# Holding TensorE to the order of the source in a two-layer encoder, while the other engines stay with the scheduler

## The chip, the core and the metric

The kernel runs on one core of one Trainium2 chip. The metric is the device time of one execution in microseconds (us), lower is better. The profile is one execution, recorded by the hardware profiler. Engines are named as it names them: PE (TensorE, matmuls), PEld (its weight loads), DVE (VectorE), ACT (ScalarE), POOL (GpSimd), SP (SyncE, which issues most loads).

## What is computed

Two layers of a streaming encoder over 256 tokens of width 1024, in float32:

```python
for l in range(DEPTH):                                   # 2
    mod = (cond @ ada_w[l] + ada_b[l])[:, None, :]
    sh1, sc1, g1, sh2, sc2, g2 = jnp.split(mod, 6, axis=-1)
    h = rmsnorm(x, norm1_g[l]) * (1 + sc1) + sh1
    x = x + g1 * hybrid_mixer(h, cos, sin, w_in[l], b_in[l], rel_bias[l], w_branch[l], w_out[l])
    h = rmsnorm(x, norm2_g[l]) * (1 + sc2) + sh2
    x = x + g2 * swiglu(h, w_ffn_in[l], w_ffn_out[l])
return rmsnorm(x, final_g)
```

The mixer projects `h` by `w_in` (6733 columns) and runs three kinds of attention on it: over the best 64 keys of each query by an indexer (branch 0), over a band with a relative bias (branch 1), and with a cumulative forget-gate bias (branch 2). Each is projected to width 1024, gated and summed.

## The kernel before

**Products.** A float32 weight is split into a high and a low part (`whi`, made by ACT in L187; `wlo`, the rest, made by DVE in L188), and so are the activations (`hT`, buffer 108 high and 109 low in the program). A product is three matmuls into one PSUM tile: high by high, high by low, low by high. They stand in L316, L317 and L318 where the activation is the stationary side (128 x up to 512 results), and in L450, L451 and L452 where the weight is (128x256 results). A *piece* is two of the eight 128-row steps of one block of weight columns.

**Sources of order.** The Python code writes instructions in one long sequence. It already mixes work: `beat(ns)` is called after a few matmuls with their rough length, and steps the generators of attention pairs, evacuations and `ada_mac` when their pauses (`yield 7000`) are over. The scheduler then fixes an order for each engine. It may move an instruction past others of its engine if, by its own reckoning, the earlier one would wait. Each engine runs its instructions in the order that it was given.

**Start.** `start()` (from L1022) normalizes `x`, then takes the first four blocks of `w_in` (`qi` 512 columns, `kwv` 456, `fb` and `fc` 512 each) two row steps at a time. A step `kt` needs `hT` of that step: `modulate(kt)` makes it (ACT `h` in L1042 and the high part in L1045, DVE the low part in L1046) once DVE has finished the dot products of `ada_w` for it (`ada_mac`, L340).

**Pairs of branch 2.** `pair` calls `forget_bias` for each of its two heads and then `scores` for both:

```python
            ps = ps_x()
            for t in range(T):
                nc.tensor.transpose(ps[:, t * P:(t + 1) * P], nF[:, t, h:h + 1].to_broadcast([P, P]), ident)
            nc.vector.scalar_tensor_tensor(b[:, REG[0]], ps[:, 0:P], F[:, 0, h:h + 1], ...)
            nc.vector.scalar_tensor_tensor(b[:, REG[1]], ps[:, 0:S], F[:, 1, h:h + 1], ...)
```

The transposes are L739, the two DVE instructions L740 and L742. `scores` is L646 and L648, and DVE reads its result in L770. All of these tiles are `ps_x` tiles, of which there are four: the transposes of a second pair can start only when L742 has read the tile of the first, and its scores when L770 has.

**Loads.** `w_in`, `ada_w` and the other weights come through one SP queue into four `raw` buffers, in the order of a list. A buffer is free again when its second L188, or its second L340, is through.

Of the kernel before, what the change touches and what calls it, by code (L numbers as in the profile page):

```python
# [11 lines left out]
F32 = mybir.dt.float32  # L12
# [6 lines left out]
P = 128  # L19
D = 1024  # L20
S = 256
T = 2
DEPTH = 2
# [3 lines left out]
FKT = FFN // P  # L27
# [67 lines left out]
def hybrid_encoder(ctx: ExitStack, tc: tile.TileContext, a):  # L95
    nc = tc.nc

    RAW_BUFS, SPLIT_BUFS = 4, 6
    OUT_HELD, OUT_EXTRA, FFN_HELD, FFN_EXTRA = 8, 4, 8, 3
    START_BLOCKS, START_RAWS, START_EXTRA = 4, 6, 4  # L100
# [13 lines left out]
    def ps_x():  # L114
        return psum.tile([P, 512], F32, tag="x", name="ps_x", bufs=4)

    def flat(src, off, dims):
        return bass.AP(tensor=src.tensor, offset=src.offset + off, ap=dims)
# [9 lines left out]
    piece_pools, piece_out = [(splitp, SPLIT_BUFS, 1 << 30), None], [0, 0]  # L128
# [8 lines left out]
    raw_out, raw_bufs, on_ada = [0, 0], [RAW_BUFS, START_RAWS], [None]  # L137
    start_pool = [None]
# [737 lines left out]
    def out_proj(l):  # L876
        pso = {(t, cb): (ps_gemm(512),) for t in range(T) for cb in range(2)}
        items = [(cb, kg * 4 + 2 * p) for kg in range(2) for cb in range(2) for p in range(2)]
        open_items(pso, items[:-OUT_HELD], KT - 1, hT)
        items = [(cb, kt, get()) for cb, kt in items[-OUT_HELD:]]  # L880
        drain()
        return closing(l, "g1", pso, items, KT - 1, hT, [Norm(t, l, 2) for t in range(T)], [FFN_BLOCKS[0][1]] * 2)
# [12 lines left out]
    def ffn_in(l, fp, sp, first):  # L895
        aT = [fp.tile([P, FKT, S], F32R, name=f"aT{i}", bufs=1) for i in range(2)]
        aV = [v.rearrange("p k (t q) -> p t k q", t=T) for v in aT]

        def act(k0, n, sg):
            yield 7000  # L900
            for t in range(T):
                pt = ps_x()
                for j in range(n):
                    nc.tensor.transpose(pt[:, j * P:(j + 1) * P], sg[t][:, j * P:(j + 1) * P], ident)
                evac_split(pt[:, :n * P].rearrange("p (k q) -> p k q", q=P), aV[0][:, t, k0:k0 + n],
                           aV[1][:, t, k0:k0 + n])
                yield 1000

        def silu(ps):
            out = []  # L910
            for p in ps:
                g = sp.tile([P, 512], F32, tag="sg", name="sg", bufs=4)
                nc.scalar.activation(g, p, AF.Silu)
                out.append(g)
            return out

        for c0, w in FFN_BLOCKS:
            k0 = c0 // P
            if first:
                sg = silu(first.pop(0))  # L920
                psu = first.pop(0)
                for t in range(T):
                    nc.vector.tensor_mul(sg[t], sg[t], psu[t])
                e = act(k0, w // P, sg)
                spawn(e, next(e))
                continue
            sg = silu(block_T(w))
            psu = block_T(w)
            for i, g in enumerate(sg):
                nc.vector.tensor_mul(g, g, psu[i])  # L930
                hi, lo = [v[:, k0 + 2 * i:k0 + 2 * i + 2, :].rearrange("p k q -> p (k q)") for v in aT]
                nc.scalar.activation(hi, g, AF.Copy)
                nc.vector.tensor_sub(lo, g, hi.bitcast(F32))
        drain()
        return aV
# [141 lines left out]
    @contextmanager  # L1077
    def more_pieces(name, bufs, n):
        with tc.tile_pool(name=name, bufs=bufs) as pool:
            piece_pools[1] = (pool, bufs, got[0] + n)  # L1080
            yield
            piece_pools[1] = None
            assert piece_out[1] == 0

    with tc.tile_pool(name="start", bufs=1) as start_pool[0]:
        piece_pools[1] = (start_pool[0], START_EXTRA, 4 * START_BLOCKS)
        first = start()
        piece_pools[1] = None
        assert piece_out[1] == 0 and raw_out[1] == 0
    for l in range(DEPTH):  # L1090
        last = l + 1 == DEPTH
        with tc.tile_pool(name=f"mix{l}", bufs=2) as ap:
            mixer(l, ap, first)
        with more_pieces(f"mid{l}", OUT_EXTRA, 8 + 8):
            first = out_proj(l)
        with tc.tile_pool(name=f"ffn{l}", bufs=2) as fp:
            with tc.tile_pool(name=f"silu{l}", bufs=4) as sp:
                aV = ffn_in(l, fp, sp, first)
            if last:
                gain = fp.tile([P, D], F32, name="gain", bufs=1)  # L1100
                nc.gpsimd.dma_start(gain, flat(a["final_g"], 0, [[0, P], [1, D]]))
            with more_pieces(f"end{l}", FFN_EXTRA, FKT + (0 if last else 8)):
                if last:
                    ffn_out(l, aV, None, [Final(t) for t in range(T)])
                else:
                    first = ffn_out(l, aV, [len(c) for _, c in IN_BLOCKS[:2]], [Norm(t, l + 1, 1) for t in range(T)])


# [65 lines left out]
```

## Time and profile before

| | |
|---|---|
| device time, median of 3 runs | 869.18 us (867.4 to 869.26) |
| the profiled execution | 868.24 us |
| its span, first to last instruction | 866.5 us |
| PE busy | 840.3 us |
| DVE busy | 635.6 us |
| ACT busy | 479.2 us |
| PE matmuls in the trace | 5918 |

The span is what the trace covers; 1.74 us of the profiled execution lie outside it. Busy time of PE includes the modelled end of each matmul, so short pauses between matmuls don't show in it; they show in the distance between the starts of two matmuls. An L number is a line of the kernel.

### The profile page before, as it was taken

What the parts mean: (1) busy time and instruction counts of PE and PEld (TensorE: products, weight loads), DVE (VectorE), ACT (ScalarE), POOL (GpSimd) and SP (SyncE); (2) the same over time, 40 slices, a digit from 0 to 9 for tenths busy, and PEclk for the clock granted to TensorE, in tenths of its full rate; (3) what the DMA queues carried; (4) which work ended last, traced back from release to release, by engine and by line L of the source; (5) the groups of instructions that cost most, each with busy time, mean ns of one, the idle gap of its engine ahead of it and who ended that gap; (6) DMA issues with size and microseconds to landing.
All of it is one profiled execution on the core that took longest, in us unless ns stands there. A gap on an engine that the chain in (4) does not pass through costs nothing.

```text
span 866.5 us, 14949 instructions
## 1 busy us (share of the span) xinstructions
PE 840.3 (97%) x5918; PEld 779.1 (90%) x5918; DVE 635.6 (73%) x1090; ACT 479.2 (55%) x811; POOL 53.5 (6%) x100
## 2 busy tenths in 40 slices
PE   3999999999999999999999999999999999999996
PEld 2999898999878999998879999898998799999886
DVE  6985988969886776697465786787898755647734
ACT  5556856764574544364354576767456544445522
POOL 3010310000010000000012013000000000000001
PEclk9999999999999999999999999999999999999999
DMA  9977566668836775689444456377795556636801
GB/s 351 415 271 219 195 234 230 227 246 351 307 130 258 263 282 211 213 324 364 149 178 126 139 191 243 147 279 253 279 375 187 202 219 225 219 118 251 326 12 48
DMA packets 32437, 200.48 MB, mean 231 GB/s; under 512 B 3872, under 2 KB 3888, under 8 KB 13680
## 3 DMA queue, kind: packets, MB, share of 16 engines
q1 hardware_dynamic: 30960, 195.16, 61.8%
q0 software_dynamic: 1264, 4.38, 1.7%
q8 instruction: 46, 0.75, 0.3%
q14 instruction: 23, 0.19, 0.1%
q10 hardware_dynamic: 144, 0.00, 0.0%
HBM read 198.48 MB, written 1.05 MB: 230 GB/s over the span
## 4 chain that ended last, share of the span: by engine, by line
PE 83%; DVE 9%; ACT 3%; issue 2%; DMA 2%; POOL 1%; POOLq 0%; DVEq 0%
PE ps_g L450 15%; PE ps_g L452 15%; PE ps_g L451 15%; PE ps_g L316 10%; PE ps_g L317 10%; PE ps_g L318 10%; DVE wlo L188 4%; DMA raw<-in_ada_w_dram 1%; PE ps_x L648 1%; PE ps_x L790 1%; PE ps_x L450 1%; POOL var L379 1%; PE ps_x L451 1%; PE ps_x L452 1%; PE ps_x L646 1%
## 5 line engine op out<-in xcount | busy, mean ns | idle before, releaser
L188 DVE TENSOR_TENSOR wlo<-raw,whi 128x1024 fp32r<-128x1024 f32 (+5 forms) x300 | 332.2, 1123 | 134.7 <-ACT whi L187 133.7
L187 ACT ACTIVATE whi<-raw 128x1024 fp32r<-128x1024 f32 (+5 forms) x300 | 288.0, 974 | 249.5 <-PE ps_g L451 135.5
L450 PE MATMUL ps_g<-hT,whi 128*128 128x256 f32 x1056 | 301.9, 286 | 0.9 <-DVE pr L572 0.9
L452 PE MATMUL ps_g<-hT,wlo 128*128 128x256 f32 x1056 | 297.9, 282 | 0.0
L451 PE MATMUL ps_g<-hT,whi 128*128 128x256 f32 x1056 | 297.3, 282 | 0.0
L450 PEld LDWEIGHTS ps_g<-hT,whi 128*128 128x128 f32 x1056 | 198.9, 188 | 5.0 <-issue 4.9
L451 PEld LDWEIGHTS ps_g<-hT,whi 128*128 128x128 f32 x1056 | 199.2, 189 | 0.4 <-issue 0.3
L452 PEld LDWEIGHTS ps_g<-hT,wlo 128*128 128x128 f32 x1056 | 198.8, 188 | 0.3 <-issue 0.3
L340 DVE CUSTOM_DVE_ANT_0 raw<-raw,cond,adab 128x1024 f32<-128x1024 f32 x96 | 122.8, 1299 | 26.5 <-DMA raw<-in_ada_w_dram 26.5
L316 PE MATMUL ps_g<-whi,hT 128*128 128x512 f32 (+4 forms) x320 | 118.6, 373 | 0.9 <-ACT hT L1045 0.9
L317 PE MATMUL ps_g<-wlo,hT 128*128 128x512 f32 (+4 forms) x320 | 117.3, 367 | 0.0
L318 PE MATMUL ps_g<-whi,hT 128*128 128x512 f32 (+4 forms) x320 | 116.5, 366 | 0.0
L316 PEld LDWEIGHTS ps_g<-whi,hT 128*128 128x128 f32 x320 | 60.5, 190 | 11.1 <-issue 2.3
L317 PEld LDWEIGHTS ps_g<-wlo,hT 128*128 128x128 f32 x320 | 60.7, 190 | 7.9 <-DVE wlo L188 0.3
L318 PEld LDWEIGHTS ps_g<-whi,hT 128*128 128x128 f32 x320 | 60.6, 189 | 7.8
L316 PE MATMUL ps_g<-whi,aT 128*128 128x512 f32 (+1 forms) x176 | 66.4, 377 | 0.0
L317 PE MATMUL ps_g<-wlo,aT 128*128 128x512 f32 (+1 forms) x176 | 66.3, 377 | 0.0
L318 PE MATMUL ps_g<-whi,aT 128*128 128x512 f32 (+1 forms) x176 | 66.2, 376 | 0.0
L379 POOL TENSOR_SCALAR var<-sq 128x1 f32<-128x1 f32 x10 | 6.5, 647 | 601.6 <-ACT xn L376 598.5
L774 ACT ACTIVATE lg<-lg,mx 128x128 f32<-128x128 f32 x64 | 28.3, 443 | 19.5 <-DVE mx L770 19.4
L318 PEld LDWEIGHTS ps_g<-whi,aT 128*128 128x128 f32 x176 | 33.1, 188 | 6.1
L317 PEld LDWEIGHTS ps_g<-wlo,aT 128*128 128x128 f32 x176 | 33.1, 188 | 6.0
(210 smaller groups left out, 959.0 us busy)
## 6 DMA issues: line engine op xcount, KB each, us to landing
raw<-in_ada_w_dram SPq DMA_DIRECT2D x48, 1024.0 KB, 5.6
raw<-in_w_ffn_in_dram SPq DMA_DIRECT2D x40, 1024.0 KB, 4.9
raw<-in_w_in_dram SPq DMA_DIRECT2D x30, 1024.0 KB, 5.3
raw<-in_w_ffn_out_dram SPq DMA_DIRECT2D x20, 1024.0 KB, 7.0
raw<-in_w_branch_dram SPq DMA_DIRECT2D x12, 768.0 KB, 4.6
raw<-in_w_in_dram SPq DMA_DIRECT2D x16, 512.0 KB, 8.7
raw<-in_w_out_dram SPq DMA_DIRECT2D x8, 1024.0 KB, 6.9
raw<-in_w_in_dram SPq DMA_DIRECT2D x8, 768.0 KB, 5.1
```

The lines of the kernel that those rows point to most:

```text
L187: nc.scalar.activation(hi, r, AF.Copy)
L188: nc.vector.tensor_sub(lo, r, hi.bitcast(F32))
L316: nc.tensor.matmul(ps, lh, wh, start=start, stop=False)
L317: nc.tensor.matmul(ps, lh, wl, start=False, stop=False)
L318: nc.tensor.matmul(ps, ll, wh, start=False, stop=stop)
L340: nc.vector.tensor_tensor_reduce(out=wj, in0=wj, in1=cond, op0=OP.mult, op1=OP.add, scale=ngain[:, l, int(name[2]) - 1, k:k + 1] if name[: ...
L379: nc.gpsimd.tensor_scalar(v, self.sq[:, i:i + 1], EPS if i == 0 else self.v, None, op0=OP.add)
L450: nc.tensor.matmul(ps, wh[:, c], ah, start=first, stop=False, skip_group_check=True)
L451: nc.tensor.matmul(ps, wh[:, c], al, start=False, stop=False, skip_group_check=True)
L452: nc.tensor.matmul(ps, wl[:, c], ah, start=False, stop=stop, skip_group_check=True)
L646: nc.tensor.matmul(p[:, 0:P], q[:, 0:P], k[:, 0:P], start=True, stop=True)
L774: nc.scalar.activation(lg[:, REG[t]], lg[:, REG[t]], AF.Exp, bias=mx[:, t:t + 1], scale=-1.0, accum_out=sm[:, t:t + 1])
```

## The change

The whole emission of the program, from `start()` on, is put into a block that takes PE away from the scheduler: PE's instructions keep the order in which the source writes them. The order of the other engines is still the scheduler's, made anew with PE's order given.

```diff
-    with tc.tile_pool(name="start", bufs=1) as start_pool[0]:
-        piece_pools[1] = (start_pool[0], START_EXTRA, 4 * START_BLOCKS)
-        first = start()
...
+    with tc.manual_schedule(engines={mybir.EngineType.PE}):
+        with tc.tile_pool(name="start", bufs=1) as start_pool[0]:
+            piece_pools[1] = (start_pool[0], START_EXTRA, 4 * START_BLOCKS)
+            first = start()
...
+        for l in range(DEPTH):
+            last = l + 1 == DEPTH
+            with tc.tile_pool(name=f"mix{l}", bufs=2) as ap:
+                mixer(l, ap, first)
+            with more_pieces(f"mid{l}", OUT_EXTRA, 8 + 8):
+                first = out_proj(l)
...
```

Nothing else is edited; the rest of the block is the old code, indented. Of PE's 5752 matmuls in the program (the score matmuls and some others stand twice in the trace) 80 stand at another place than before: 22 at the very start; six groups of three a little later in `start()`, where the L316 of the second token tile stood ahead of an L317 or L318 of the first; and 40 around the second pair of branch 2, 21 of them in layer 0 and 19 in layer 1. SP and POOL keep their order. On ACT four short stretches change, on DVE twelve.

PE, first matmuls of the program, right behind the sixteen transposes of `xn`. Rows with 128x512 are block `qi`, with 128x456 `kwv`, with 128x256 `fb`; `hT_108` is the high part of the activations, `hT_109` the low. Before:

```order
L316 MATMUL ps_g<-whi,hT_108 128x512
L317 MATMUL ps_g<-wlo,hT_108 128x512
L316 MATMUL ps_g<-whi,hT_108 128x512
L318 MATMUL ps_g<-whi,hT_109 128x512
L317 MATMUL ps_g<-wlo,hT_108 128x512
L318 MATMUL ps_g<-whi,hT_109 128x512
L316 MATMUL ps_g<-whi,hT_108 128x456 x2
L450 MATMUL ps_x<-hT_108,whi 128x256
L451 MATMUL ps_x<-hT_109,whi 128x256
L317 MATMUL ps_g<-wlo,hT_108 128x456
L318 MATMUL ps_g<-whi,hT_109 128x456
```

Now:

```order
L316 MATMUL ps_g<-whi,hT_108 128x512
L317 MATMUL ps_g<-wlo,hT_108 128x512
L318 MATMUL ps_g<-whi,hT_109 128x512
L316 MATMUL ps_g<-whi,hT_108 128x512
L317 MATMUL ps_g<-wlo,hT_108 128x512
L318 MATMUL ps_g<-whi,hT_109 128x512
L316 MATMUL ps_g<-whi,hT_108 128x512
L317 MATMUL ps_g<-wlo,hT_108 128x512
L318 MATMUL ps_g<-whi,hT_109 128x512
L316 MATMUL ps_g<-whi,hT_108 128x512
L317 MATMUL ps_g<-wlo,hT_108 128x512
L318 MATMUL ps_g<-whi,hT_109 128x512
```

The first six are row step 0 of `qi` in both. Then eight matmuls of `kwv` and `fb` on row step 0 came next; now the six of `qi` on row step 1 do, and the eight come behind them.

PE, second pair of branch 2 in layer 0, right behind the scores of the first pair (`hT`, `whi`, `wlo` rows are block `g3`). Before:

```order
L450 MATMUL ps_g<-hT_108,whi 128x256
L451 MATMUL ps_g<-hT_109,whi 128x256
L452 MATMUL ps_g<-hT_108,wlo 128x256
L450 MATMUL ps_g<-hT_108,whi 128x256
L451 MATMUL ps_g<-hT_109,whi 128x256
L739 MATMUL ps_x<-ident,F_1515 128x128 x2
L452 MATMUL ps_g<-hT_108,wlo 128x256
L450 MATMUL ps_g<-hT_108,whi 128x256
L451 MATMUL ps_g<-hT_109,whi 128x256
L452 MATMUL ps_g<-hT_108,wlo 128x256
L450 MATMUL ps_g<-hT_108,whi 128x256
L739 MATMUL ps_x<-ident,F_1515 128x128 x2
```

Now:

```order
L739 MATMUL ps_x<-ident,F_1517 128x128 x4
L646 MATMUL ps_x<-fc_738,fc_737 128x128 x2
L648 MATMUL ps_x<-fc_738,fc_737 128x256 x2
L450 MATMUL ps_g<-hT_108,whi 128x256
L451 MATMUL ps_g<-hT_109,whi 128x256
```

The four transposes and four score matmuls of the pair now stand together, and the 13 matmuls of `g3` that stood among them (five, five, and three ahead of the scores) come behind. In layer 1 the same happens with 11.

DVE, layer 0, between the scores of the last head of branch 2 and L797, behind which PE's next scores wait (L340 is `ada_mac`, one row with its accumulator's read; `y` is the gated sum of the branches, whose `ps_g` PE makes). Before:

```order
L828 SCALAR_TENSOR_TENSOR y_699<-gate,ps_g 128x512
L340 ISA raw,mg_1704<-raw,cond,adab 128x1024
L340 ISA mg_1704 128x1
L776 RECIPROCAL sm<-sm 128x2
L188 TENSOR_TENSOR wlo<-raw,whi 128x1024 x2
L828 SCALAR_TENSOR_TENSOR y_700<-gate,ps_g 128x512 x2
L188 TENSOR_TENSOR wlo<-raw,whi 128x1024 x3
L340 ISA raw,mg_1704<-raw,cond,adab 128x1024
L340 ISA mg_1704 128x1
```

Now:

```order
L340 ISA raw,mg_1706<-raw,cond,adab 128x1024
L340 ISA mg_1706 128x1
L828 SCALAR_TENSOR_TENSOR y_701<-gate,ps_g 128x512
L776 RECIPROCAL sm<-sm 128x2
L188 TENSOR_TENSOR wlo<-raw,whi 128x1024 x2
L828 SCALAR_TENSOR_TENSOR y_702<-gate,ps_g 128x512 x2
L188 TENSOR_TENSOR wlo<-raw,whi 128x1024 x2
L340 ISA raw,mg_1706<-raw,cond,adab 128x1024
L340 ISA mg_1706 128x1
L188 TENSOR_TENSOR wlo<-raw,whi 128x1024
```

Two L340 moved ahead by one place each. Most other changes on DVE are of this kind: an L340 ahead of one to four instructions that wait for PE; the longest is one L340 in layer 1, ahead by 21.

## Rows read from the trace of the kernel before

**Rows 1.** The page: the span; shares of the chain that ended last, by engine.

```profile
span 866.5 us, 14949 instructions
...
PE 83%; DVE 9%; ACT 3%; issue 2%; DMA 2%; POOL 1%; POOLq 0%; DVEq 0%
```

**Rows 2.** The timeline of PE at the start: start, length, instruction, idle time before.

```profile
18.23 0.79 PE L316 MATMUL ps_g<-whi,hT 128*128 128x512 f32 x1 [0.91 <-ACT hT L1045]
18.82 0.63 PE L317 MATMUL ps_g<-wlo,hT 128*128 128x512 f32 x1
...
20.95 0.96 PE L316 MATMUL ps_g<-whi,hT 128*128 128x456 f32 x2
...
22.36 0.75 PE L317 MATMUL ps_g<-wlo,hT 128*128 128x456 f32 x1
...
23.23 0.36 PE L317 MATMUL ps_g<-wlo,hT 128*128 128x456 f32 x1
...
23.64 0.39 PE L316 MATMUL ps_g<-whi,hT 128*128 128x512 f32 x1
...
25.02 0.37 PE L316 MATMUL ps_g<-whi,hT 128*128 128x456 f32 x1
...
26.26 0.28 PE L452 MATMUL ps_x<-hT,wlo 128*128 128x256 f32 x1
```

**Rows 3.** The timeline of DVE and ACT in the same stretch.

```profile
21.20 2.24 DVE L188 TENSOR_TENSOR wlo<-raw,whi 128x912 fp32r<-128x912 f32 x2
21.96 0.42 ACT L1045 ACTIVATE hT<-h 128x256 fp32r<-128x256 f32 x1
23.36 0.42 DVE L1046 TENSOR_TENSOR hT<-h,hT 128x256 fp32r<-128x256 f32 x1
```

**Rows 4.** Windows: a stretch with busy time and instructions of PE, PEld, DVE, ACT, POOL.

```profile
300.00:350.00 50.00, 50.00 (x422) 50.00 (x421) 34.82 (x42) 23.72 (x28) 0.00 (x0) 1.00 0.69 245
```

**Rows 5.** The chain that ended last, in order of time, near 91 us: start, length, what.

```profile
91.13 0.19 PE ps_g L318
...
91.34 0.85 ACT whi L187
```

**Rows 6.** The timeline of PE around the second pair of branch 2, layer 0.

```profile
132.39 0.39 PE L450 MATMUL ps_g<-hT,whi 128*128 128x256 f32 x1
...
133.85 0.40 PE L739 MATMUL ps_x<-ident,F 128*128 128x128 f32 x2 [0.60 <-DVE lg L742]
...
136.37 0.39 PE L451 MATMUL ps_g<-hT,whi 128*128 128x256 f32 x1
```

**Rows 7.** The timeline of DVE in the same stretch.

```profile
133.88 0.47 DVE L742 SCALAR_TENSOR_TENSOR lg<-ps_x,F,causal 128x256 f32<-128x256 f32 x1
...
135.03 0.42 DVE L770 CUSTOM_DVE_ANT_0 lg<-ps_x,lg 128x256 f32<-128x256 f32 x1
```

**Rows 8.** The timeline of PE around the same pair of layer 1.

```profile
543.00 0.39 PE L450 MATMUL ps_g<-hT,whi 128*128 128x256 f32 x1
...
546.20 0.39 PE L452 MATMUL ps_g<-hT,wlo 128*128 128x256 f32 x1
```

**Rows 9.** Layer 0 behind the pair: DVE's timeline, its window, PE's timeline.

```profile
150.98 0.69 DVE L828 SCALAR_TENSOR_TENSOR y<-gate,ps_g 128x512 f32<-128x512 f32 x1 [0.51 <-PE ps_g L823]
151.00:162.40 11.40, 11.40 (x97) 11.13 (x95) 11.37 (x16) 7.62 (x12) 0.00 (x0) 1.00 0.60 217
162.18 0.38 PE L646 MATMUL ps_x<-kaT,qaT 64*128 64x128 f32 x2
162.88 0.37 PE L646 MATMUL ps_x<-kaT,qaT 64*128 64x128 f32 x1 [0.32 <-DVE oh L797]
```

**Rows 10.** Layer 1 behind the pair: the timeline of DVE, then of PE.

```profile
557.55 1.29 DVE L340 CUSTOM_DVE_ANT_0 raw<-raw,cond,adab 128x1024 f32<-128x1024 f32 x1 [3.45 <-DMA raw<-in_ada_w_dram]
592.41 0.48 PE L646 MATMUL ps_x<-kaT,qaT 64*128 64x128 f32 x2
593.67 0.37 PE L646 MATMUL ps_x<-kaT,qaT 64*128 64x128 f32 x1 [0.77 <-DVE ol L795]
```

More of the change, by code (lines that the diff above doesn't have):

```diff
@@ L1083, in more_pieces @@
             assert piece_out[1] == 0
-    with tc.tile_pool(name="start", bufs=1) as start_pool[0]:
-        piece_pools[1] = (start_pool[0], START_EXTRA, 4 * START_BLOCKS)
-        first = start()
[L1088 to L1102, printed above, removed]
-                if last:
-                    ffn_out(l, aV, None, [Final(t) for t in range(T)])
-                else:
-                    first = ffn_out(l, aV, [len(c) for _, c in IN_BLOCKS[:2]], [Norm(t, l + 1, 1) for t in range(T)])
+    with tc.manual_schedule(engines={mybir.EngineType.PE}):
+        with tc.tile_pool(name="start", bufs=1) as start_pool[0]:
+            piece_pools[1] = (start_pool[0], START_EXTRA, 4 * START_BLOCKS)
+            first = start()
+            piece_pools[1] = None
+            assert piece_out[1] == 0 and raw_out[1] == 0
+        for l in range(DEPTH):
[4 more added lines that the diff above has]
+                first = out_proj(l)
+            with tc.tile_pool(name=f"ffn{l}", bufs=2) as fp:
+                with tc.tile_pool(name=f"silu{l}", bufs=4) as sp:
+                    aV = ffn_in(l, fp, sp, first)
+                if last:
+                    gain = fp.tile([P, D], F32, name="gain", bufs=1)
+                    nc.gpsimd.dma_start(gain, flat(a["final_g"], 0, [[0, P], [1, D]]))
+                with more_pieces(f"end{l}", FFN_EXTRA, FKT + (0 if last else 8)):
+                    if last:
+                        ffn_out(l, aV, None, [Final(t) for t in range(T)])
+                    else:
+                        first = ffn_out(l, aV, [len(c) for _, c in IN_BLOCKS[:2]], [Norm(t, l + 1, 1) for t in range(T)])
```

## The prediction

> **What bounds the kernel now.** I read the page first: the span, and by which engine the chain that ended last runs. PE has 83% of that chain, DVE 9% [rows 1], and over the program PE is rarely idle. So the reader should expect every microsecond in which PE waits, and did not wait before, to be found again at the end, unless PE would have waited a little later anyway. I then compared the old and the new order of PE. It is the same for all but 80 of 5752 matmuls, so this is a change at three places: the first microseconds, and the second pair of branch 2 in each layer. Last I read the timelines of PE, DVE and ACT at these places, for what each displaced matmul had been covering, and of the stretches behind them, for waits that could take the loss up.
>
> The old order is close to the source because the source already mixes work. What the scheduler had added was just this: where a matmul's operand was not there yet, later matmuls that were ready went first. The change takes these away. It removes no instruction and adds none.
>
> **The start.** The first six matmuls (128x512) are the same set in both orders and run from 18.23 us on; the next start is at 20.95 [rows 2]. They run at PE's lower clock: five of them take from 18.82 to 20.95, 0.43 us each, against 0.23 each for the six from 23.64 to 25.02. These are the two levels, 1.2 and 2.4 GHz; the change lies just ahead of 23.23, from where two matmuls take 0.41 us up to 23.64 [rows 2]. At 20.95 the old order went on with `kwv` and `fb` on row step 0. The new one wants row step 1 of `hT`, whose high part ACT ends at 21.96 + 0.42 = 22.38 and whose low part DVE ends at 23.36 + 0.42 = 23.78, since two L188 stand ahead of it [rows 3]. Neither waits for PE, and neither engine's order changes here, so I keep their times. Then:
>
> - PE waits from 20.95 to about 22.42, that is 1.47 us;
> - it runs L316 and L317 of step 1, 0.59 us for the first behind a wait (18.23 to 18.82) and 0.43 for the next [rows 2], up to 23.44;
> - L318 needs the low part: it waits to about 23.82, 0.38 us more;
> - from there 4 matmuls of 512, 12 of 456 and 2 of 256 columns remain until the place that PE reached at 26.26 before [rows 2].
>
> What these 18 cost hangs on the clock. At the higher level: 4 x 0.23 + 12 x 0.207 + 2 x 0.118 = 3.64 us (0.207 from the six between 25.02 and 26.26 [rows 2]; 0.118 is 50 us over 422 matmuls, nearly all of 256 columns [rows 4]). That ends at 27.46, **1.2 us** late. At the lower level throughout: 0.59 + 3 x 0.43 + 12 x 0.38 + 2 x 0.21 = 6.86 us (0.38 and 0.21 are 0.43 times 456/512 and 256/512), which ends at 30.68, **4.4 us** late. Before, the engine worked from 18.23 with one pause, ahead of the L317 at 22.36 that waited for the first of these L188 [rows 2, 3], and then its clock rose. The two new waits lie in the microseconds just ahead of that point, so I expect the rise later than before, but no reason to expect it only behind all 18. I take the middle, **2.8 us**. The six groups of three later in the start cost nothing: PE reaches them later by then and their `wlo` no earlier, so the operand that the old order stepped around is there; if it isn't, each costs one wait of a few tenths.
>
> Does this shift reach the end? From 23.64 to 91.31 the chain is PE's own. Where it leaves PE, at 91.34, it does so for an ACT L187 that begins when PE's last L318 of a block ends [rows 5]: ACT waits for a piece's buffer, and PE's lateness is handed on to ACT and DVE. I count it whole.
>
> **The second pair of branch 2, layer 0.** The scores of the first pair end at 132.39 and the stretch ends with the L451 at 136.37 [rows 6]. In it PE waited once, 0.60 us ahead of L739 [rows 6], and covered the rest of DVE's time with 13 matmuls of `g3`. The transposes and scores cannot start earlier than before: the second transposes need the tile that L742 leaves at 133.88 + 0.47 = 134.35, the last scores the tile that L770 leaves at 135.03 + 0.42 = 135.45 [rows 7]; four score matmuls and their pause behind it bring PE to about 136.4 again. So the 13 come on top: 13 x 0.118 = **1.53 us**. Here a rule of the skill could be held against the sum. The waiting L739 at 133.85 had L452 of the same block right behind it, whose piece the matmuls ahead had already read, and yet PE stood idle [rows 6]. The Trainium skill, "TensorE: Matmul & The Clock Gate", section "Step-by-step: what each phase is for", says that PE pulls weight loads ahead of matmuls, while the matmuls stay in program order. If matmuls too were pulled ahead, the 13 would cost nothing; the row agrees with the page's limit.
>
> Part of the 1.53 can be taken up behind it. PE waits for DVE at 162.88 in any case; its two matmuls before began at 162.18 and took 0.22 to issue, so it waited 0.48 [rows 9]. DVE is full from 151.0 to 162.4 (11.37 of 11.40 us), and had waited 0.51 for PE ahead of the L828 at 150.98 [rows 9]. The new order of DVE puts an L340 ahead of that L828, which fills this wait: DVE falls 1.53 - 0.51 = 1.02 behind, PE 1.53 - 0.48 = 1.05. I take **1.05**; the upper end is 1.53, if L340's load isn't there.
>
> **The same in layer 1.** From 543.00 to 546.20 [rows 8], with 11 displaced matmuls: 11 x 0.118 = **1.30 us**. Behind it DVE's time is set by a load, not by PE: the L340 at 557.55 had waited 3.45 us for it [rows 10]. PE's next wait for DVE is at 593.67; PE was there at 592.41 + 0.22, so it waited 1.04 us [rows 10]. If DVE keeps its time, PE loses only 1.30 - 1.04 = 0.26; if DVE falls as far behind as PE, 1.30. Between them DVE runs splits that wait for PE through ACT, which delay it, and L340s that moved ahead into these waits, which give it back. I take the middle, **0.8 us**.
>
> **The other changes on DVE and ACT** are cost at nothing. A split delayed by an L340 (1.29 us [rows 10]) is hidden by the pieces made ahead; where that cover were gone, each such place would cost up to 1.3 us.
>
> **The sum** is 2.8 + 1.05 + 0.8 = 4.65 us on the profiled execution: 868.24 + 4.65 = 872.9. That execution is 0.94 us below the median of the runs shown, 869.18. I give 873.4, half of that added. The bounds of the sum are 1.2 + 1.05 + 0.26 = 2.5 and 4.4 + 1.53 + 1.30 = 7.2 us.
>
> **The rivals.**
>
> *A. The waits are swallowed (no change).* PE's new waits stand where old ones stood or are followed by them: 0.60 at 133.85, 0.48 at 162.88, 1.04 at 593.67 [rows 6, 9, 10] make 2.1 us. If DVE kept its times of before, these would come off, and the start would be at its lower end: 1.2 + 1.53 + 1.30 - 2.1 = 1.9, 870.2, and less still if DVE's stretch near 91 us did not shift. For it speaks that DVE is full in these stretches; against it that ACT's L187 at 91.34 waits for PE [rows 5].
>
> *B. Faster, by DVE's new order.* An L340 ends earlier, its `raw` buffer is free earlier, and the next load in the one queue starts earlier. The price: DVE waits 3.45 us for such a load at 557.55 [rows 10], and the waits of PE for DVE at 162.88 and 593.67 (0.48 + 1.04 = 1.5 us) would be gone. It decides only if the three places cost PE less than 1.5 us together, so with the start near nothing: about 867.5. Against it: the order of DVE at 557.55 itself and ahead of it is unchanged in layer 1, and the start's operands are late by clear rows [rows 3].
>
> *C. Slower still.* The clock stays low beyond the 18 matmuls, or an L340 moved ahead of work that PE needs waits for its load. One more microsecond on every four at the lower clock, or 1.3 us at each such place: 876 and more.
>
> *D. PE steps around a waiting matmul by itself.* Then the order given is not the order run, and nothing changes: 868.2. The 0.60 us idle at 133.85 with work ready behind [rows 6] speaks against it.
>
> **How the numbers follow.** 0.2% is 1.7 us, about what a measurement of this kernel can tell from no change. Forecast (2.5 to 6 us more): 0.70. A: 0.14, D: 0.02, B: 0.05, C: 0.09. All but 2 in 10 lie from 870.0 to 877.0: the low end is the sum's lower bound on the profiled execution less half a microsecond, the high end the upper bound, 868.24 + 7.2 = 875.4, on the median and a little of C. Within the forecast alone I would say 871 to 875.5. Slower takes the forecast, C and a little of A: 0.80. Same: the rest of A and D, 0.15. Faster: B, 0.05.
>
> **What would show it.** Right: PE's timeline has a wait of about 1.5 us for ACT L1045 near 21 us and a shorter one for DVE L1046, matmuls of 512 columns still 0.43 us apart behind them, and the L452 of 26.26 at about 29. Around the second pairs L739 waits about 1.4 us for L742 with no `ps_g` matmul between the pair's transposes and its scores, and the stretch is 1.5 and 1.3 us longer. The wait at 162.88 stays about as it is, that at 593.67 shrinks. Wrong: if the block `fc` ends no later than before, or if waits of PE for DVE or ACT that stand in the old profile are gone in sum by as much as the new ones bring.

## The result, and the profile after

The changed kernel takes 875.18 us (median of 6 executions, 874.28 to 876.1), the kernel before, run beside it, 867.58 us (867.26 to 869.26, 6 executions). The ratio is 1.0081, with a 95% interval of 1.0071 to 1.0092: slower, by some 7 us. The forecast was 873.4, in a range of 870.0 to 877.0. Below, "before" and "after" are these two kernels, and "lateness" is the difference between the starts of one and the same matmul in two traces.

The page of after: its span, the busy time, and the chain that ended last, by engine and by line.

```profile
span 873.6 us, 14945 instructions
PE 842.7 (96%) x5918; PEld 780.2 (89%) x5918; DVE 636.3 (73%) x1090; ACT 480.3 (55%) x811; POOL 53.4 (6%) x100
PE 84%; DVE 7%; ACT 4%; issue 2%; DMA 2%; POOL 1%; POOLq 0%; DVEq 0%; ACTq 0%
```

The chain looks as before [rows 1]; a share does not show where 7 us were lost. The waits of PE do (what waited, for what, us in all, times, the longest):

```profile
PE ps_g L316 <- ACT hT L1045: 3.3, 2, 2.4
PE ps_x L739 <- DVE lg L742: 3.1, 4, 1.5
PE ps_g L318 <- DVE hT L1046: 0.7, 1, 0.7
PE ps_x L646 <- DVE ol L795: 0.3, 1, 0.3
```

The first three are the forecast's waits: the start's two, and L739 around the second pairs, which waited once for 0.60 us before [rows 6]. L646 for L797 at 162.88 [rows 9] is gone from the list, and L646 for L795 shrank from 0.77 [rows 10] to 0.33.

The timeline of PE in after, the start (start, length, instruction, idle time before):

```profile
17.92 0.50 PE L316 MATMUL ps_g<-whi,hT 128*128 128x512 f32 x1 [0.92 <-ACT hT L1045]
...
19.13 0.39 PE L317 MATMUL ps_g<-wlo,hT 128*128 128x512 f32 x1
19.36 0.40 PE L318 MATMUL ps_g<-whi,hT 128*128 128x512 f32 x1
22.11 0.50 PE L316 MATMUL ps_g<-whi,hT 128*128 128x512 f32 x1 [2.35 <-ACT hT L1045]
22.45 0.40 PE L317 MATMUL ps_g<-wlo,hT 128*128 128x512 f32 x1
23.52 0.50 PE L318 MATMUL ps_g<-whi,hT 128*128 128x512 f32 x1 [0.68 <-DVE hT L1046]
23.85 0.49 PE L316 MATMUL ps_g<-whi,hT 128*128 128x512 f32 x1
24.14 0.63 PE L317 MATMUL ps_g<-wlo,hT 128*128 128x512 f32 x1
24.57 0.63 PE L318 MATMUL ps_g<-whi,hT 128*128 128x512 f32 x1
25.00 0.59 PE L316 MATMUL ps_g<-whi,hT 128*128 128x456 f32 x1
...
28.81 0.28 PE L452 MATMUL ps_x<-hT,wlo 128*128 128x256 f32 x1
```

In this execution the clock was already high at the first matmuls of 512 columns (0.23 us from 19.13 to 19.36), so PE came early to row step 1 and waited 2.35 us instead of 1.47; then it fell, and 512 columns took 0.43 us again from 24.14 on. The L452 that started at 26.26 before [rows 2] starts at 28.81. The same order of waits, another course of the clock, nearly the same loss.

Windows of after (stretch, length; busy time and instructions of PE, PEld, DVE, ACT, POOL; PEclk, the granted clock; DMA share; GB/s), two of the start, one around layer 0's pair, three around layer 1's:

```profile
17.20:23.90 6.70, 2.96 (x10) 1.61 (x11) 6.70 (x14) 4.40 (x7) 0.00 (x0) 1.00 1.01 414
24.10:27.30 3.20, 3.20 (x10) 2.70 (x9) 3.20 (x6) 0.00 (x0) 0.00 (x0) 0.50 1.02 407
...
134.00:141.00 7.00, 5.13 (x38) 3.69 (x37) 6.95 (x30) 3.74 (x16) 0.00 (x0) 1.00 0.21 88
546.00:549.50 3.50, 2.00 (x15) 0.98 (x13) 3.50 (x17) 1.31 (x6) 0.00 (x0) 1.00 0.00 0
549.70:553.00 3.30, 3.30 (x16) 2.65 (x13) 3.24 (x14) 3.30 (x14) 0.00 (x0) 0.50 0.02 5
553.20:560.00 6.80, 6.80 (x61) 6.80 (x60) 3.27 (x5) 5.43 (x14) 0.00 (x0) 1.00 0.80 307
```

The same stretch of layer 1 in before:

```profile
543.00:553.00 10.00, 9.94 (x82) 9.30 (x81) 8.21 (x32) 8.57 (x29) 0.00 (x0) 1.00 0.27 93
```

What the reader is to see: behind layer 1's pair the granted clock is 0.50 for a stretch, the 1.2 GHz level, in which PE never paused. Nothing of the kind stands in before, nor behind layer 0's pair here, where L739 waited 1.50 and 0.25 us against 1.13 and 0.25 in layer 1. The timeline of after at layer 1's pair:

```profile
545.88 0.60 PE L648 MATMUL ps_x<-fc,fc 64*128 64x256 f32 x4
547.61 0.40 PE L739 MATMUL ps_x<-ident,F 128*128 128x128 f32 x2 [1.13 <-DVE lg L742]
548.26 0.40 PE L739 MATMUL ps_x<-ident,F 128*128 128x128 f32 x2 [0.25 <-DVE lg L742]
...
550.91 0.42 PE L451 MATMUL ps_g<-hT,whi 128*128 128x256 f32 x1
551.13 0.41 PE L452 MATMUL ps_g<-hT,wlo 128*128 128x256 f32 x1
...
553.05 0.29 PE L452 MATMUL ps_g<-hT,wlo 128*128 128x256 f32 x1
553.18 0.28 PE L450 MATMUL ps_g<-hT,whi 128*128 128x256 f32 x1
```

Matmuls of 256 columns stand 0.21 to 0.22 us apart up to 553.05, then 0.12 to 0.13.

The lateness of after against before, read from equal matmuls, adds up to the difference of the spans (873.6 less 866.5, 7.1):

| where (us of before) | lateness | gained there |
|---|---|---|
| first transposes, 13.64 | -0.31 | |
| behind the start, 27 to 60 | 2.57 | +2.88 |
| ahead of layer 0's pair, 120 to 131 | 2.57 | 0 |
| behind it, 139 to 142 | 4.21 | +1.64 |
| behind the wait at 162.88 | 3.57 | -0.61 (from 4.18) |
| ahead of layer 1's pair, 520 to 540 | 3.41 | -0.16 |
| behind it, 549 to 553 | 6.74 | +3.33 |
| behind the wait at 593.67 | 6.54 | -0.20 |
| last 20 us | 7.07 | +0.53 |

So the question for the experiments was: does each place cost this by itself, and what is the 3.33 of layer 1, where 1.3 had been forecast?

### The profile page after: what moved, and what is told of

It is laid out like the page before. It is cut to its first block, busy times and chain, and to the rows that moved or that the text cites. A ratio compares the mean times of both kernels' runs of the same rounds, so it can differ in the third digit from the quotient of the medians.

```text
span 873.6 us, 14945 instructions
## 1 busy us (share of the span) xinstructions
PE 842.7 (96%) x5918; PEld 780.2 (89%) x5918; DVE 636.3 (73%) x1090; ACT 480.3 (55%) x811; POOL 53.4 (6%) x100
## 3 DMA queue, kind: packets, MB, share of 16 engines
HBM read 198.48 MB, written 1.05 MB: 228 GB/s over the span
## 4 chain that ended last, share of the span: by engine, by line
PE 84%; DVE 7%; ACT 4%; issue 2%; DMA 2%; POOL 1%; POOLq 0%; DVEq 0%; ACTq 0%
PE ps_g L450 15%; PE ps_g L452 15%; PE ps_g L451 15%; PE ps_g L316 10%; PE ps_g L318 10%; PE ps_g L317 10%; DVE wlo L188 3%; ACT whi L187 1%; PE ps_x L790 1%; DMA raw<-in_ada_w_dram 1%; PE ps_x L648 1%; PE ps_x L783 1%; POOL var L379 1%; DVE raw L340 1%; PE ps_x L450 1%
## 5 line engine op out<-in xcount | busy, mean ns | idle before, releaser
L450 PE MATMUL ps_g<-hT,whi 128*128 128x256 f32 x1056 | 303.1, 287 | 0.9 <-DVE pr L572 0.9
L452 PE MATMUL ps_g<-hT,wlo 128*128 128x256 f32 x1056 | 298.6, 283 | 0.0
L450 PEld LDWEIGHTS ps_g<-hT,whi 128*128 128x128 f32 x1056 | 199.8, 189 | 5.3 <-issue 5.2
L452 PEld LDWEIGHTS ps_g<-hT,wlo 128*128 128x128 f32 x1056 | 199.4, 189 | 0.0
L340 DVE CUSTOM_DVE_ANT_0 raw<-raw,cond,adab 128x1024 f32<-128x1024 f32 x96 | 122.9, 1300 | 31.7 <-DMA raw<-in_ada_w_dram 31.5
L316 PE MATMUL ps_g<-whi,hT 128*128 128x512 f32 (+4 forms) x320 | 119.1, 372 | 3.3 <-ACT hT L1045 3.3
L318 PE MATMUL ps_g<-whi,hT 128*128 128x512 f32 (+4 forms) x320 | 117.3, 367 | 0.7 <-DVE hT L1046 0.7
L317 PE MATMUL ps_g<-wlo,hT 128*128 128x512 f32 (+4 forms) x320 | 117.2, 366 | 0.0
L316 PEld LDWEIGHTS ps_g<-whi,hT 128*128 128x128 f32 x320 | 60.7, 190 | 13.8 <-ACT hT L1045 4.1
L318 PEld LDWEIGHTS ps_g<-whi,hT 128*128 128x128 f32 x320 | 60.6, 190 | 9.2 <-DVE hT L1046 1.5
L317 PEld LDWEIGHTS ps_g<-wlo,hT 128*128 128x128 f32 x320 | 60.7, 190 | 7.4
L316 PE MATMUL ps_g<-whi,aT 128*128 128x512 f32 (+1 forms) x176 | 66.4, 377 | 0.0
L317 PE MATMUL ps_g<-wlo,aT 128*128 128x512 f32 (+1 forms) x176 | 66.3, 377 | 0.0
L318 PE MATMUL ps_g<-whi,aT 128*128 128x512 f32 (+1 forms) x176 | 66.2, 376 | 0.0
L318 PEld LDWEIGHTS ps_g<-whi,aT 128*128 128x128 f32 x176 | 33.1, 188 | 6.1
L317 PEld LDWEIGHTS ps_g<-wlo,aT 128*128 128x128 f32 x176 | 33.2, 188 | 6.0
L316 PEld LDWEIGHTS ps_g<-whi,aT 128*128 128x128 f32 x176 | 33.1, 188 | 6.0
```

What stands on the lines that cost most here:

```text
L316: nc.tensor.matmul(ps, lh, wh, start=start, stop=False)
L317: nc.tensor.matmul(ps, lh, wl, start=False, stop=False)
L318: nc.tensor.matmul(ps, ll, wh, start=False, stop=stop)
L340: nc.vector.tensor_tensor_reduce(out=wj, in0=wj, in1=cond, op0=OP.mult, op1=OP.add, scale=ngain[:, l, int(name[2]) - 1, k:k + 1] if name[: ...
L450: nc.tensor.matmul(ps, wh[:, c], ah, start=first, stop=False, skip_group_check=True)
L452: nc.tensor.matmul(ps, wl[:, c], ah, start=False, stop=stop, skip_group_check=True)
```

## The experiments

Each kernel was timed against before on the same chip, so the ratios compare best; the us of before differ a little from chip to chip (867.5, 867.7 and 868.3 in the three sets). The ratio is not the quotient of the medians: for `filled_wait` the medians give 1.0044, for after 1.0088.

| kernel | us, median (range, executions) | ratio, 95% interval |
|---|---|---|
| after | 875.18 (874.28 to 876.1, 6) | 1.0081 [1.0071, 1.0092] |
| `start_only` | 870.43 (868.47 to 871.04, 7) | 1.0028 [1.0017, 1.0039] |
| `layers_only` | 873.04 (872.0 to 873.17, 5) | 1.0057 [1.0045, 1.0070] |
| `pair_covered` | 870.02 (868.55 to 870.83, 8) | 1.0026 [1.0016, 1.0036] |
| `start_by_step` | 873.21 (871.22 to 873.92, 5) | 1.0058 [1.0046, 1.0071] |
| `both_rewritten` | 868.16 (867.35 to 869.83, 11) | 1.0008 [0.9999, 1.0017] |
| `filled_wait` | 871.52 (871.23 to 872.56, 5) | 1.0051 [1.0037, 1.0065] |
| `layer1_only` | 869.47 (868.12 to 870.95, 8) | 1.0018 [1.0006, 1.0030] |
| `before_covered` | 868.28 (867.88 to 869.95, 11) | 1.0009 [1.0000, 1.0018] |
| `layer0_only` | 870.91 (868.35 to 874.39, 12) | 1.0031 [1.0019, 1.0044] |
| `start_filled` | 870.6 (869.02 to 871.23, 11) | 1.0018 [1.0009, 1.0027] |
| `all_filled` | 872.84 (871.09 to 873.53, 5) | 1.0048 [1.0036, 1.0060] |

### One place at a time: `start_only`, `layers_only`, `layer0_only`, `layer1_only`

The block that keeps PE's order is put around a part of the program only (unchanged lines are left out here and in the next code blocks, and the comments are added).

```diff
+    with tc.manual_schedule(engines={mybir.EngineType.PE}):     # start_only: around start()
+    with tc.manual_schedule(engines={mybir.EngineType.PE}):     # layers_only: around the loop over l
+        with tc.manual_schedule(engines={mybir.EngineType.PE}) if l == 0 else nullcontext():  # layer0_only
```

`layer1_only` has `l == 1` in the last line.

> Only start() keeps PE to the source; both layers stay with the scheduler, and PE's order there is that of before. Theory (the losses add up place by place): the trace of after is 2.55 us late behind the start, and this lateness is handed on whole, so 867.6 + 2.5 = 870.1 us, the granted clock in layer 1 stays at its high level, and L739 there waits as in before. Rival 1 (the start is swallowed by later waits): 867.6 to 868.3. Rival 2 (the fall of the clock in layer 1 comes from the shift of the whole program, not from the pair's wait): the clock falls there here too, 871.5 to 873.

> start() stays with the scheduler; both layers keep PE to the source. Theory: layer 0 costs 1.0 us net (1.76 at the pair less 0.72 taken up at the wait for L797), layer 1 about 3 (1.3 of displaced matmuls and about 1.7 of matmuls at the lower clock behind the pair), the rest of after's drift 0.5: 867.6 + 4.5 = 872.1 us, and the granted clock falls for about 3.4 us behind layer 1's second pair, as in after. Rival: the fall hangs on the phase that the start gave, not on the pair; then no fall and 869.5 to 870.3.

> Only layer 0 keeps PE to the source. Theory: 1.76 us at the pair with the clock high, 3.0 with a fall behind it, less 0.7 taken up at the wait for L797: 868.6 us in executions without a fall and 870 in those with one. Rival (layers_only showed a further wait of 0.9 us of L355 behind layer 0, and this goes with the new order by itself): 1 us more in either case, 869.6 and 871.

> Only layer 1 keeps PE to the source. Theory: the pair costs 1.35 us with the clock high and 2.95 where the clock falls behind it, and 0.4 is taken up at the wait near 593 us: 868.5 us in executions without a fall, 870.1 in those with one, the median between. Rival (layer 1 loses because layer 0 and the start come late, not by itself): 867.6 with no more than 0.3 added.

The start alone gives 1.0028, the layers alone 1.0057: together 0.85%, after has 0.81%. Layer 0 alone gives 1.0031 and layer 1 alone 1.0018, 0.49% together. The losses add up, within the intervals. In `start_only` the lateness behind the start (2.21 us, 2.55 from the first transposes) is 2.02 ahead of layer 1's pair and 1.93 behind it: it is handed on nearly whole (1.70 in the last 20 us), it does not bring the clock down in layer 1, and the six groups of three later in the start cost nothing that shows.

The traces of the layers say more. Windows of `layers_only`, whose clock fell behind layer 0's pair and not behind layer 1's (543 to 553):

```profile
131.00:134.60 3.60, 1.94 (x14) 0.96 (x12) 3.60 (x16) 0.81 (x4) 0.00 (x0) 1.00 0.33 139
134.80:138.00 3.20, 3.20 (x14) 2.55 (x15) 3.15 (x15) 3.20 (x13) 0.00 (x0) 0.50 0.00 0
543.00:553.00 10.00, 8.45 (x67) 6.93 (x66) 8.68 (x33) 6.52 (x23) 0.00 (x0) 1.00 0.04 17
```

Windows of `layer0_only`, with a longer fall at the same place, and one in the start, although the start's order there is that of before:

```profile
23.40:26.70 3.30, 3.30 (x9) 2.66 (x9) 3.30 (x8) 0.00 (x0) 0.00 (x0) 0.50 1.01 401
132.00:135.90 3.90, 2.20 (x18) 1.23 (x16) 3.90 (x12) 0.68 (x2) 0.00 (x0) 1.00 0.50 210
136.10:142.70 6.60, 6.60 (x29) 5.89 (x30) 4.46 (x22) 5.07 (x21) 0.00 (x0) 0.50 0.21 43
```

The lateness gained across a pair goes with that:

| clock behind the pair | layer 0 | layer 1 |
|---|---|---|
| high throughout | 1.64 (after), 1.60 (`start_by_step`) | 1.25 (`layer1_only`), 1.87 (`layers_only`) |
| low for one stretch, some 3.4 us | 3.04 (`layers_only`) | 3.33 (after) |
| low for about twice that | 4.40 (`layer0_only`) | 4.85 (`start_by_step`) |

So a pair with the new order costs 1.3 to 1.9 us, and a fall of the clock adds about 1.4 to 2.1, or twice as much. The waits are not the same everywhere: the two high-clock values of layer 1 differ by 0.6 us, and so does the wait of L739, in `layer1_only` and then in `layers_only`:

```profile
543.40 0.40 PE L739 MATMUL ps_x<-ident,F 128*128 128x128 f32 x2 [0.57 <-DVE lg L742]
...
546.80 0.40 PE L739 MATMUL ps_x<-ident,F 128*128 128x128 f32 x2 [1.18 <-DVE lg L742]
```

Whether the clock falls differs from place to place and from execution to execution: it fell behind four of the eight pairs in these five traces. In the four without a fall L739's longest wait was 0.57, 1.18, 1.44 and 1.50 us, in the four with one 1.13, 1.25, 1.36 and 1.45. The times vary too. Of `layer1_only`'s eight executions four took 868.1 to 868.8 and four 870.15 to 870.95, and `layer0_only` spreads over 6 us: 868.35 to 869.31 at a mean granted clock of 0.998, 870.27 to 870.95 at 0.996, 871.36 to 874.39 at 0.991 to 0.995 (its trace is of the slowest, 874.39). Not all of such a spread is the new order's: before itself took 868.8 to 869.8 in 5 of 24 executions beside `layer1_only` and 869.1 to 870.1 in 6 of 23 beside `layer0_only`, the others at most 868.6.

The rival of `layers_only` (no fall without the start's shift, 869.5 to 870.3) is out, as is that of `layer1_only`. But the expectation of `layers_only` missed in two ways: it was 0.9 us low, and the fall came behind layer 0's pair and not behind layer 1's, so where it comes may still hang on the course of the execution ahead of it. Its trace also shows a wait that had not been forecast, 0.9 us of L355 for DVE's L795 behind layer 0. `layer0_only` was to tell whether this comes with the new order. Its trace has 0.4 us of it and `start_by_step` none, so it is not constant; I did not find what decides it. The times expected for `layer0_only`, with or without it, end at 871; 5 of its 12 executions took longer, and a fall of double length was in neither.

### The waits covered in the source: `pair_covered`, `start_by_step`, `both_rewritten`, `before_covered`

```diff
             lgs, biases = [], []
+            if br == 2 and hs[0] == 2:
+                yield 1200                  # two groups of six g3 matmuls come ahead
             for h in hs:
...
+            if br == 2 and hs[0] == 2:
+                yield 600                   # and one ahead of the scores
             for lg, bias, ps in zip(lgs, biases, scores(*[operands(br, h) for h in hs])):
```

> All of PE in the order of the source, but the source puts two groups of six g3 matmuls ahead of the second pair's transposes and one ahead of its scores, in both layers. Theory (PE's waits at the pairs are the cost of the layers, and the clock falls because of them): both pairs cost what they cost in before, the clock stays high in layer 1, only the start is left: 870.1 us. Rival (the layers lose by DVE's and ACT's changed order, L340 ahead of work that PE waits for, or the fall of the clock is unrelated to the pair's wait): 872.5 or more, up to 875.

With the pairs covered, 1.0026 is left, which is `start_only`'s 1.0028. The waits of PE in `pair_covered`:

```profile
PE ps_g L316 <- ACT hT L1049: 2.2, 2, 1.3
PE ps_g L318 <- DVE hT L1050: 0.7, 1, 0.7
PE ps_x L739 <- DVE lg L742: 0.2, 1, 0.2
```

L739 waits 0.2 us instead of 3.1, the granted clock of its trace never falls in the layers, and DVE's and ACT's orders, which also differ from before, cost nothing that shows. The rival (872.5 or more) is out.

In `start_by_step` the loop of `start()` takes row step 0 of `qi`, `kwv` and `fb`, then row step 1 of the three (`row_step` is the old loop body as a function; a loop that advanced `ada_mac` ahead of each later piece falls away with it):

```diff
+                if p == 0 and i < EARLY:            # EARLY = 3
+                    held.append(get())
...
+                    row_step(i, 0, held[-1])
...
+                    if i == EARLY - 1:
+                        for j, pc in enumerate(held):
+                            row_step(j, 1, pc)
+                            done(pc)
+                    continue
```

> All of PE in the order of the source, but the source takes row step 0 of qi, kwv and fb ahead of row step 1, as the scheduler did. Theory (the start's loss is the two waits for hT of step 1): the waits of 2.35 and 0.68 us are gone, 2.5 us less than after, 872.6 us; layer 1 still shows the fall of the clock. Rival (what the scheduler gained in the start is the order of the two token tiles within a step, which stays as in the source here): 874.5 to 875.2.

1.0058, 0.23% below after: as the theory had it, though by a detour. PE's first wait in the start that is not in after:

```profile
21.94 0.47 PE L317 MATMUL ps_g<-wlo,hT 128*128 128x456 f32 x1 [2.10 <-DVE wlo L188]
```

The waits for `hT` of step 1 are gone, and PE waits 2.10 us for the first `wlo` of `kwv` instead; still it leaves the start no later than in before (lateness -0.35 against -0.43 at the first transposes). That is the wait that before has ahead of its L317 at 22.36 [rows 2]: DVE sets the time here, and before's order has useful work in it up to then. The fall behind layer 1's pair was there, and longer (the 4.85 above).

> All of PE in the order of the source, and the source rewritten at both places: row step 0 of qi, kwv and fb ahead of row step 1 in the start, and g3 matmuls around the second pairs. Theory (these two places are the whole of the loss): no change against before, 867.0 to 868.5 us. Rival (some loss lies elsewhere, in DVE's and ACT's order or in the six groups of three in the start): 869.5 or more.

It has both edits, `pair_covered`'s and `start_by_step`'s. 1.0008, with 1 inside the interval, whose upper end is 1.5 us: keeping PE to the source costs nothing that can be told once the source has cover at these two places (the start and the pairs). By this the loss is in them.

> The kernel before, all engines with the scheduler, with only the second pairs of branch 2 rewritten so that 12 g3 matmuls stand ahead of their transposes and 6 ahead of their scores. Theory (the scheduler had already covered these waits but for 0.6 us a layer): 866.5 to 867.5 us, at most 1 us less than before. Rival (the later second pair delays the attention work behind it): 868 and more.

`before_covered` applies the pair's edit to before, with PE left to the scheduler: 1.0009, no gain. The expectation, up to 1 us less than before, missed; the time is the rival's, 868 and more. Its trace, like that of `both_rewritten`, moves work but ends where before ends (span 866.6 and 866.5). None of the kernels beats before.

### Work instead of idling: `filled_wait`, `start_filled`, `all_filled`

To part the wait from the clock, PE is given work that brings nothing. The tile `zr` holds zeros, and the product is added to the open `g3` tile.

```diff
+    def fill(n):
+        for _ in range(n):
+            nc.tensor.matmul(open_ps[0], zr, hT[0][:, :, 0, :], start=False, stop=False, skip_group_check=True)
...
+            if br == 2 and hs[0] == 2:
+                fill(11)                    # ahead of the second pair's forget_bias
...
+            if br == 2 and hs[0] == 2:
+                fill(2)                     # ahead of its scores
```

> As after, with 11 matmuls by a tile of zeros ahead of the second pair's transposes and 2 ahead of its scores, in both layers: they add zero to the open g3 tile, so PE works through the waits but has no useful work done there. DVE's and ACT's orders are those of after. Theory (the fall of the clock is brought by PE standing idle at the pair): the granted clock stays high behind both pairs; each pair still costs the 1.3 to 1.8 us of its wait, but not the up to 1.6 more of the fall: 873.5 us, and 874.2 at most. Rival 1 (the fall is unrelated to the idle time, it lies in the small matmuls of the scores or is a matter of chance): falls as in after, 875.2. Rival 2 (the fill is longer than the wait): 875.5 and more, without a wait ahead of L739.

The timeline of PE in `filled_wait` at layer 1's pair, where L462 is the fill and L750, L657 and L659 are after's L739, L646 and L648:

```profile
544.16 0.60 PE L659 MATMUL ps_x<-fc,fc 64*128 64x256 f32 x4
544.69 1.57 PE L462 MATMUL ps_g<-hT,zr 128*128 128x256 f32 x11
546.10 0.91 PE L750 MATMUL ps_x<-ident,F 128*128 128x128 f32 x4
546.76 0.48 PE L462 MATMUL ps_g<-hT,zr 128*128 128x256 f32 x2
```

And its windows over both pairs:

```profile
134.00:141.00 7.00, 6.75 (x52) 5.76 (x51) 6.46 (x30) 5.49 (x22) 0.00 (x0) 1.00 0.02 4
546.00:553.00 7.00, 6.88 (x55) 6.05 (x54) 6.67 (x28) 6.31 (x24) 0.00 (x0) 1.00 0.11 18
```

The clock stays at 1.00 behind both. The pairs still cost 1.65 and 1.88 us in lateness: the zeros win no time back. But the kernel, with 26 matmuls more, is at 1.0051 against after's 1.0081, and the intervals don't meet. The difference, 0.30% of 867.6 or 2.6 us by the ratios (3.8 by the medians), holds what the clock took at the pairs over these executions, and with it what the start took, whose clock varies in both kernels; the medians don't part the two. The five executions have a mean granted clock of 0.997 to 0.999, after's six 0.992 to 0.996 (a mean takes in the start, and the last microseconds, where the clock falls in every trace). In the traces of the four kernels in which PE hardly idles at the pairs (this one, `all_filled`, `pair_covered`, `both_rewritten`) the clock fell behind none of eight; where PE idles in the new order, behind four of eight. The ten pairs in these traces that have the scheduler's order say the same: L739's longest wait there is 0.76 us, and the clock fell behind none. None of 18 against four of eight is hardly chance, so the idling brings the fall, though not each time. I expected 873.5 and it came to 871.5, so the expectation missed by 2 us, to the better side: of the 4.1 us between the two profiled executions (875.33 and 871.23) 3.33 - 1.88 = 1.45 lie at layer 1's pair and 1.56 in the start, whose clock rose near 21.3 here and stayed up.

In the start the same remedy was too small:

```diff
                 for k in range(2):
+                    if p == 0 and i == 0 and k == 1:
+                        for _ in range(4):
+                            nc.tensor.matmul(first[0][1], zr, pc[0][:, 0], start=False, stop=False)
```

> As start_only, with four matmuls of 512 columns by a tile of zeros ahead of row step 1 of qi, which add zero to its open tile: PE works where it stood idle for hT. Theory (half of the start's loss is the clock, which rises later or falls again because PE stands idle): the granted clock rises by 23 us or earlier and stays high, the start costs the 1.2 to 1.5 us of the waits alone, 868.8 to 869.2 us. Rival (the operands set the time, whatever the clock): 870.4 as in start_only, or more where the four outlast the wait.

> As after, with the zero matmuls of filled_wait at the pairs and those of start_filled in the start. Theory (the waits alone, with no fall of the clock, cost 1.3 in the start, 1.0 in layer 0 and 0.8 in layer 1): 870.7 us, 4.5 less than after although PE runs 30 matmuls more. Rival (the start's part is set by operands): 871.5 as filled_wait.

Both missed: 870.6 where 868.8 to 869.2 had been expected, 872.84 where 870.7 had. In `start_filled`'s trace the four take 1.10 us, PE still waits 1.43 and 0.67, and the clock falls as in after:

```profile
19.64 1.10 PE L1065 MATMUL ps_g<-whi,zr 128*128 128x512 f32 x4
22.16 0.50 PE L316 MATMUL ps_g<-whi,hT 128*128 128x512 f32 x1 [1.43 <-ACT hT L1050]
...
23.57 0.50 PE L318 MATMUL ps_g<-whi,hT 128*128 128x512 f32 x1 [0.67 <-DVE hT L1051]
...
24.70 0.63 PE L318 MATMUL ps_g<-whi,hT 128*128 128x512 f32 x1
25.12 0.58 PE L316 MATMUL ps_g<-whi,hT 128*128 128x456 f32 x1
```

Against `start_only` the ratios (1.0018 and 1.0028) have intervals that overlap, so whether the fill helps is not settled. Five of `start_filled`'s eleven executions took 869.0 to 869.6 at a mean granted clock of 0.998 to 0.999 and six 870.6 to 871.2 at 0.996 to 0.997, so the expected time may come where the clock stays up, but the trace is of one of the six; `all_filled` (1.0048) is not told apart from `filled_wait`. What the start costs at a high clock is shown by two other traces: in `pair_covered` and `filled_wait` the clock rises near 21.2 and does not fall, and the lateness gained in the start is 1.34 and 1.32 us. With the clock low up to 26.2 (`start_only`) it is 2.55, with the fall of after's trace 2.88. The clock also has a price there without the new order: `layer0_only`, whose start is before's, gained 1.25 us against before's in the start of its trace, with the fall at 23.4 shown above.

## Why the prediction was right, and where a term was off

**The number.** 875.18 us lies in the range, but the change is larger than the forecast: 7.6 us between the medians, and 7.1 between the two profiled executions, where the sum gave 4.65 and its upper bound was 7.2. That the time lies well inside the range is in part luck: the forecast started from 869.18, the median of three executions, and before took 867.58 beside after.

**What bounds the kernel.** Right. Each wait that PE gained at the three places is found again at the end, less 0.6 us at 162.88 and 0.2 at 593.67.

**The start, 2.8 us (1.2 to 4.4).** Right in size: 2.88 in the trace, 2.9 between the medians of `start_only` and before (870.43 less 867.54). The bounds held too, 1.3 being the least that a trace shows. The picture of the clock was only one of several: I had it rise late, once, and so it did in `start_only`'s trace (26.2); in after's it had risen before the first of these matmuls and fell again, so that the size came out of another course there, which is luck. That the waits by themselves delay the rise is not borne out: in `pair_covered` and `filled_wait` PE waited for `hT` as well, and the clock rose near 21.2, earlier than in before, where it rose just ahead of 23.23 [rows 2].

**Layer 0's pair, 1.05 us net.** The waits were sized rightly: 1.64 at the pair (forecast 1.53), 0.61 taken up at 162.88 (forecast 0.48), 1.03 net in after's trace. I had said that this wait of PE would stay, since DVE would come as late; it is gone. No fall of the clock stood in the term, and in the traces of `layers_only` and `layer0_only` it costs 1.4 and 2.8 us more here.

**Layer 1's pair, 0.8 us net.** This is the term that was mis-sized. "11 x 0.118 = 1.30" was 1.25 in `layer1_only`, but 1.9 where layer 0 had the new order as well (`layers_only`, `filled_wait`; in the first L739 waited 1.18 us instead of 0.57, and why L742 came later there stays open), and in after it was 3.33, of which about 1.7 is the clock: in the 3.4 us at half speed PE does what would take 1.7. And of the 1.04 us that PE's wait at 593.67 could take up I assumed half. That wait did shrink by 0.44, to 0.60; but PE had lost another 0.25 at the L783 near 587, so that 0.2 net was taken up. In all 3.1 net in after's trace.

**The other changes on DVE and ACT, nothing.** Right as far as can be told: `both_rewritten` has such changes and costs 0.5 us by the medians, with 1 inside its interval.

**The rivals.** A took the waits to be swallowed; some 0.8 us of them were. B and D are out: the kernels in which DVE's order changes and PE loses nothing are no faster (1.0008, 1.0009), and PE stands idle with work ready behind the waiting instruction, now at 547.61 as well. C had the right mechanism, a clock that stays low, but looked for it in the start and behind a late L340; it came behind the pairs, and in after's start as a fall. Its price, one more microsecond on every four at the lower clock, was too small: 512 columns take 0.43 us there and 0.23 at the higher one [rows 2], which is 1.9 on four. The sum of 4.65 us lacks the clock at the pairs above all: with the 2.6 us between after and `filled_wait`, the start's share included, it would be 7.3, against 7.6 between the medians.

**Left open.** The lateness grows by 0.8 us between 700 and 781 us (the L450 of 699.97 in before comes 6.53 later, that of 773.84 comes 7.35 later) and 0.3 of it goes back by 800; no wait of PE is named there, and the other traces don't show it. The windows of before and of after between these two matmuls:

```profile
699.97:773.84 73.87, 73.87 (x625) 73.87 (x624) 44.73 (x48) 34.96 (x41) 0.00 (x0) 1.00 0.53 185
706.50:781.19 74.69, 74.69 (x625) 74.69 (x624) 44.73 (x48) 34.96 (x41) 0.00 (x0) 1.00 0.51 184
```

The same 625 matmuls take 1.1% longer, evenly over the stretch, with PE busy and the granted clock at 1.00 in both; so this 0.8 is neither a wait nor a fall of the granted clock, and nothing shows that the change made it. What decides in which execution a wait brings the clock down, the runs don't show.

## What to carry to other kernels

When an engine's order is taken from the scheduler, look for the few places where it had put ready work in front of an operand that was late; that work can be written into the source at these places, and here nothing was lost then that could be told (1.0008). Price a new wait of TensorE not only by its length: ask what the clock was and whether it can fall behind the wait, and keep a bound for this in the sum. And when a gain or a loss varies between executions of one kernel, compare their granted clocks before looking for a transfer.

## What the runs showed of the hardware that had not been expected

Waits of about 1.1 to 1.5 us with a few short ones behind them, in a program whose PE is busy for 96% of the span, were followed by a granted clock of 0.50 in some executions and not in others: at like waits, 1.00 behind layer 0's pair and 0.50 behind layer 1's in after, the other way round in `layers_only`. In the start, too, PE's wait of 2.10 us for `wlo` in `start_by_step` was not followed by a fall, and one of 1.82 us in `layer0_only` was, so the length of the wait alone does not decide it. The stretch at half speed lay behind the wait, where PE worked without a pause, so the busy share of it shows nothing. The Trainium skill, "TensorE: Matmul & The Clock Gate", section "A second HAM failure mode: psum-queue depth-cycling", tells of a kernel in which short idle moments between groups, while PSUM banks were being cycled, sent the clock back and forth. The traces here agree in so far as the waits at the pairs are waits for `ps_x` tiles, of which four are in use; the page's kernel idled frequently, this one at two places. With matmuls by zeros in the wait the clock stayed up as with useful ones (PEclk 1.00 behind both pairs in `filled_wait`, and in `pair_covered`).
